# Scores of a gated recurrence: one 128 by 128 product per chunk and level, or two of 64 by 64 in two column tiles

## The chip, the cores and the metric

The kernel runs on one core of a Trainium2 chip. The metric is the device time of one execution in microseconds (us); lower is better. Before the change, three timed executions took 2496.66, 2498.34 and 2501.14 us, with a median of 2498.34 us.

## The reference

One layer of an encoder works on two requests, 256 and 1024 tokens of width 1024. Everything is held in fp32. The layer has three blocks with layer norms between them: a token mixer, a cross attention to 256 memory tokens, and a squared-ReLU MLP. The change lies in one branch of the mixer, a recurrence with four heads of width 128 that runs over the tokens in both directions. In one direction, cut to what matters:

```python
f = lb + (1 - lb) * sigmoid(zf)          # decay of each channel and token, in (0, 1)
k = 1 - f
# state: S_t = f_t * S_(t-1) + k_t v_t^T,   output: o_t = q_t S_t
scores[t, s] = sum_d q[t, d] * k[s, d] * prod(f[s+1 .. t], d)      # s <= t, inside a chunk
o = scores @ v + (q * decay) @ S_at_chunk_start
```

The other direction is the same on flipped tokens, and the two outputs are added. Then come an RMS norm over the 128 channels and a gate.

## The kernel before, in words

All 1280 tokens of both requests (T) are handled together, as ten chunks of 128 tokens (NT = 10, P = 128). Channels lie on the 128 partitions, tokens along the free dimension. The recurrent branch is the function `hgrn`. For each head h, `proj(h)` computes the projections (f for both directions, q, and for every second head the values v), and `scan(h, ...)` computes the recurrence.

`scan` cannot form `prod(f)` for each pair of tokens, so it works by levels of doubling block size B = 1, 2, 4, ... 64 (`LEVELS`). At a level, a pair of neighbouring blocks of B tokens gets the scores between its left and its right half: keys in one half, decayed to the border, times queries in the other half, decayed from the border. One arrangement serves both directions: `ka` holds for each token the key of the direction in which it is earlier (a copy on ScalarE, line 232), and `view` reads the query array `qp` with its two planes alternating every B tokens. The product of the 128 keys of a chunk with its 128 queries (line 236) gives 128 by 128 numbers, of which only those in neighbouring blocks of size B are wanted. `copy_predicated` on VectorE (line 237) writes these into `A` with a mask of the level (`masks`), for up to four chunks in one instruction (`BATCHES`: 4, 4 and 2 chunks). Before the levels, the diagonal comes from an undecayed product (line 217) that ScalarE copies into `A` whole (line 218). After the products of a level, `qp` and `ks` are multiplied on VectorE by the decays of the blocks (lines 247 and 249), and the block decays F are multiplied in pairs (line 251).

So a head has eight rounds of ten products, in fp32. In the trace TensorE shows each fp32 product as two records, each with a weight load (LDWEIGHTS) and a matrix product (MATMUL). After the levels come the states S between chunks (transposed keys, line 276; updates, line 281; additions on VectorE, lines 285 and 288), the outputs (line 300), the norm, a transpose (line 308) and the gate (line 309).

The order of work on each engine is set when the program is built: a scheduler of the tile framework (`schedule_with_timeline_sim=True`) plays the program through with times of its own and puts instructions that are ready ahead of those that are not. Here it fills TensorE between two levels with independent products: those of the gate g of the same head (line 259 evicts them), of the two large sigmoid gates (`self.gate`) and of the next head's `proj`. They are three-term products in split fp32 ("fp32r", a high and a low part of each factor), issued by the helper lines 116 to 118. Their weights are loaded by DMA, rounded on ScalarE (line 86) and split on GpSimd (line 87).

Buffers: the products of a round go to PSUM tiles `lv` (three buffers), the state products to `ms` (two buffers). `A`, `S` and the rest of a head come from the pool `hp` with one buffer each, and are used again by the next head.

Of the kernel before, what the change touches and what calls it, by code (L numbers as in the profile page):

```python
# [10 lines left out]
F32 = mybir.dt.float32  # L11
F32R = mybir.dt.float32r
F16 = mybir.dt.float16
U8 = mybir.dt.uint8
# [6 lines left out]
P = 128  # L21
# [4 lines left out]
NT = T // P  # L26
# [11 lines left out]
LEVELS = [1, 2, 4, 8, 16, 32, 64]  # L38
# [2 lines left out]
CHUNKS = [(g, c, g * GRP + c, n) for g in range(2) for c, n in GCH]  # L41
SEQS = [(0, TP // P), (TP // P, NT)]
BATCHES = [(0, 4), (4, 8), (8, 10)]
NPRE = 3
NATT = 7
HGATES = [(0, 0, (1,)), (1, 0, (0, 1)), (0, 1, (0, 1)), (1, 1, (0, 1))]
# [21 lines left out]
class Kern:  # L68
# [98 lines left out]
    def hgrn(self, xT, hp, pj, lv, ms):  # L167
        nc, a = self.nc, self.a
        masks = self.masks
# [33 lines left out]
        def scan(h, f, ks, qp, q, v):  # L203
            nka = [0]

            def new_ka():
                nka[0] += 1
                return hw[:, 6 + nka[0] % 2]

            kd = new_ka()  # L210
            A = self.t(hp, [P, NT, P], F32, "A")
            nc.vector.tensor_tensor(kd, ks[:, 0], ks[:, 1], op=ALU.add)
            nc.vector.tensor_tensor(qp, f, q.unsqueeze(1).broadcast_to([P, 2, T]), op=ALU.mult)
            for b0, b1 in BATCHES:
                ps = self.t(lv, [P, 4, P], F32, "lv")
                for c in range(b0, b1):
                    nc.tensor.matmul(ps[:, c - b0], kd[:, c * P:(c + 1) * P], q[:, c * P:(c + 1) * P], start=True, stop=True)
                nc.scalar.copy(A[:, b0:b1], ps[:, :b1 - b0])
            F, FN = f, T
            for li, B in enumerate(LEVELS):  # L220
                nb = T // (2 * B)

                def halves(x, h0, nblk=nb, B=B):
                    if B == 1:
                        return bass.AP(tensor=x.tensor, offset=x.offset + h0 * (T + 1), ap=[x.ap[0], [2, nblk]])
                    return bass.AP(tensor=x.tensor, offset=x.offset + h0 * (T + B), ap=[x.ap[0], [2 * B, nblk], [1, B]])

                def view(x, c, n=P, B=B):
                    return bass.AP(tensor=x.tensor, offset=x.offset + c * P,
                                   ap=[x.ap[0], [2 * B, n // (2 * B)], [T + B, 2], [1, B]])  # L230
                ka = new_ka()
                nc.scalar.copy(ka.rearrange("p (n h i) -> p n h i", h=2, i=B), view(ks, 0, T))
                for b0, b1 in BATCHES:
                    ps = self.t(lv, [P, 4, P], F32, "lv")
                    for c in range(b0, b1):
                        nc.tensor.matmul(ps[:, c - b0], ka[:, c * P:(c + 1) * P], view(qp, c), start=True, stop=True)  # L236
                    nc.vector.copy_predicated(A[:, b0:b1], masks[:, li].unsqueeze(1).broadcast_to([P, b1 - b0, P]),
                                              ps[:, :b1 - b0])

                def ftot(pl, half, F=F, FN=FN, B=B, nblk=nb):  # L240
                    x = F[:, pl, half:FN:2]
                    if B == 1:
                        return x
                    return x.unsqueeze(2).broadcast_to([P, nblk, B])
                for hf in range(2):
                    x = halves(qp, hf)
                    nc.vector.tensor_tensor(x, x, ftot(hf, 1 - hf), op=ALU.mult)
                    x = halves(ks, hf)
                    nc.vector.tensor_tensor(x, x, ftot(1 - hf, 1 - hf), op=ALU.mult)
                F2 = self.t(hp, [P, 2, FN // 2], F32, f"F{li % 2}")  # L250
                nc.vector.tensor_tensor(F2, F[:, :, 0:FN:2], F[:, :, 1:FN:2], op=ALU.mult)
                F, FN = F2, FN // 2

            sg = self.t(hp, [P, T], F32, "q")
            w = self.w("wh", 4 * h + 3)
            for gi, cl, c0, n in CHUNKS:
                ps = self.t(pj, [P, 512], F32, "pj")
                self.mm_t(ps[:, :n], w, xT[gi], cl, n)
                nc.scalar.activation(sg[:, c0:c0 + n], ps[:, :n], AF.Sigmoid)
                nc.vector.tensor_tensor(sg[:, c0:c0 + n], ps[:, :n], sg[:, c0:c0 + n], op=ALU.mult)  # L260

            vh = v[:, :, (h % 2) * P:(h % 2 + 1) * P]
            S = self.t(hp, [P, 2, NT - 2, P], F32, "S")
            at = [{}, {}]
            for dr in range(2):
                order = []
                for s0, s1 in SEQS:
                    cs = list(range(s0, s1))
                    if dr:
                        cs = cs[::-1]  # L270
                    order += [(c, cs[i + 1], i > 0) for i, c in enumerate(cs[:-1])]
                for g in range(0, len(order), 4):
                    grp = order[g:g + 4]
                    pt = self.t(ms, [P, 4, P], F32, "ms")
                    for j, (c, _, _) in enumerate(grp):
                        nc.tensor.transpose(pt[:, j], ks[:, dr, c * P:(c + 1) * P], self.ident)
                    kn = self.t(hp, [P, 4, P], F32, "kn", 2)
                    nc.scalar.copy(kn[:, :len(grp)], pt[:, :len(grp)])
                    pu = self.t(ms, [P, 4, P], F32, "ms")
                    for j, (c, _, _) in enumerate(grp):  # L280
                        nc.tensor.matmul(pu[:, j], kn[:, j], vh[:, c], start=True, stop=True)
                    for j, (c, nx, inner) in enumerate(grp):
                        at[dr][nx] = len(at[dr])
                        if inner:
                            nc.vector.scalar_tensor_tensor(S[:, dr, at[dr][nx]], S[:, dr, at[dr][c]], F[:, 1 - dr, c:c + 1], pu[:, j],
                                                           op0=ALU.mult, op1=ALU.add)
                        else:
                            nc.vector.tensor_copy(S[:, dr, at[dr][nx]], pu[:, j])

            ss = self.t(hp, [P, NT], F32, "ss")  # L290
            for b0, b1 in BATCHES:
                nb = b1 - b0
                po = self.t(ms, [P, 4, P], F32, "ms")
                for c in range(b0, b1):
                    terms = [(A[:, c], vh[:, c])]
                    for dr in range(2):
                        if c in at[dr]:
                            terms.append((qp[:, 1 - dr, c * P:(c + 1) * P], S[:, dr, at[dr][c]]))
                    for j, (l, r) in enumerate(terms):
                        nc.tensor.matmul(po[:, c - b0], l, r, start=j == 0, stop=j == len(terms) - 1)  # L300
                o, s_ = A[:, b0:b1], ss[:, b0:b1]
                nc.scalar.activation(o, po[:, :nb], AF.Square)
                nc.vector.tensor_reduce(s_, o, axis=AX.X, op=ALU.add)
                self.rsqrt_pow(s_, s_, 1.0 / P, nb)
                nc.vector.tensor_tensor(o, po[:, :nb], s_.unsqueeze(2).broadcast_to([P, nb, P]), op=ALU.mult)
                pt = self.t(lv, [P, 4, P], F32, "lv")
                for j in range(nb):
                    nc.tensor.transpose(pt[:, j], o[:, j], self.ident)
                nc.vector.scalar_tensor_tensor(o, pt[:, :nb], self.gn[:, 0:1], sg[:, b0 * P:b1 * P].rearrange("p (c t) -> p c t", t=P),
                                               op0=ALU.mult, op1=ALU.mult)  # L310
                nc.gpsimd.dma_start(self.o_d[h, :, b0 * P:b1 * P], o.rearrange("p c t -> p (c t)"))
# [655 lines left out]
    def run(self, stop=99):  # L967
# [13 lines left out]
        with ExitStack() as fs:  # L981
# [10 lines left out]
                        self.load_act(self.xT[g], k, a["xT"][k][:, g * GRP:(g + 1) * GRP], GRP, mp)  # L992
            with ExitStack() as hs:
                hp = hs.enter_context(tc.tile_pool(name="hp", bufs=1, reuse_waits="tile"))
                self.masks = hp.tile([P, len(LEVELS), P], U8, name="masks")
                raw = self.t(self.rawp, [P, 1024], F32, "raw")
                nm = len(LEVELS) * P
                nc.gpsimd.dma_start(raw[:, :nm], a["masks"].rearrange("p l t -> p (l t)"))
                nc.vector.tensor_copy(self.masks.rearrange("p l t -> p (l t)"), raw[:, :nm])
                self.hgrn(self.xT, hp, pj, lv, ms)  # L1000
# [37 lines left out]
def _layout(i):  # L1038
    f = np.float32
# [48 lines left out]
    r["gnorm"] = c(A["hg_gnorm"].reshape(P, 1))  # L1088
    r["ident"] = np.eye(P, dtype=f)
    ix = np.arange(P)  # L1090
    r["masks"] = c(np.stack([((ix[:, None] // b) ^ (ix[None] // b)) == 1 for b in LEVELS], 1).astype(f))
    r["wga"], r["wgb"] = tb(col["ga"]), tb(col["gb"])
    r["wpab"] = c(np.concatenate([tb(A["w_pa"][0]), tb(A["w_pb"][0])], 2))
    r["wout"] = nb(A["w_out"][0], 2, 512)
# [28 lines left out]
```

## Time and profile before

The profiled execution took 2497.39 us, and its profile spans 2495.5 us.

| What | Value |
|---|---|
| timed executions, median | 2498.34 us |
| profiled execution, its own time | 2497.39 us |
| its span | 2495.5 us |
| TensorE products (PE) busy | 2413.9 us, 97% |
| TensorE weight loads (PEld) busy | 2238.7 us, 90% |
| VectorE (DVE) busy | 1351.6 us, 54% |
| ScalarE (ACT) busy | 850.3 us, 34% |
| GpSimd (POOL) busy | 487.7 us, 20% |
| scores of the recurrence | from 170 to 558 us after the start |

Products on TensorE overlap: the profile gives each its latency, so that the sum of their times is longer than the stretch that they fill, and the distance from one start to the next is what one costs in a row of them. In the chain of waits, a piece "x20" is a run of 20 records with its length on the clock.

### The profile page before, as it was taken

The page shows a single profiled execution, that of the slowest core. Times are in us where ns is not written, and L with a number is a line of the kernel's source. Part 1 is how long each engine was busy: PE and PEld are TensorE (multiplying, and loading weights), DVE is VectorE, ACT ScalarE, POOL GpSimd, SP SyncE. Part 2 cuts the span into 40 slices and gives each one's busy share as a digit, 9 for nine tenths or more (in the row PEclk, how much of TensorE's full clock was granted, in tenths as well). Part 3 has the DMA queues.
Part 4 walks back from the last instruction along what each step waited for, and adds up shares of the span by engine and source line. Part 5 has one row for each costly group of instructions (what it writes and reads, how often), then busy time and mean ns, then how long its engine had stood idle before and what let it go on. Part 6 is the DMA issues. An engine that isn't in the chain of part 4 may idle for free.

```text
span 2495.5 us, 36014 instructions
## 1 busy us (share of the span) xinstructions
PE 2413.9 (97%) x14940; PEld 2238.7 (90%) x14940; DVE 1351.6 (54%) x2049; ACT 850.3 (34%) x1433; POOL 487.7 (20%) x423
## 2 busy tenths in 40 slices
PE   8999999999999699999999999999999999999997
PEld 6899999999978588889899999989989889999996
DVE  5136654565888585565644444457254564444435
ACT  5222222223477574324232222223222423222220
POOL 5521221214632132222100000005321210000000
PEclk9999999999999899999999999999999999999999
DMA  8611111112256587533322232335324413222211
GB/s 294 161 35 32 44 40 37 45 33 62 62 108 131 105 147 193 185 105 114 112 70 90 73 90 73 90 99 192 126 84 136 152 46 115 76 71 76 77 57 51
DMA packets 153491, 242.73 MB, mean 97 GB/s; under 512 B 85424, under 2 KB 98752, under 8 KB 152304
## 3 DMA queue, kind: packets, MB, share of 16 engines
q1 hardware_dynamic: 133424, 193.88, 27.7%
q0 software_dynamic: 19904, 46.55, 5.7%
q8 instruction: 117, 1.92, 0.3%
q14 instruction: 46, 0.38, 0.0%
HBM read 192.82 MB, written 28.05 MB: 89 GB/s over the span
## 4 chain that ended last, share of the span: by engine, by line
PE 75%; DVE 6%; DMA 4%; ACT 2%; issue 1%; POOL 0%; POOLq 0%; SPq 0%; DVEq 0%; ACTq 0%
PE a L117 9%; PE a L118 9%; PE a L116 9%; PE a L127 8%; PE a L128 8%; PE a L129 8%; PE pj L118 2%; PE pj L116 2%; PE pj L117 2%; PE lv L236 2%; DMA act<-p 1%; PE of L485 1%; PE of L116 1%; PE of L118 1%; PE of L117 1%
## 5 line engine op out<-in xcount | busy, mean ns | idle before, releaser
L116 PE MATMUL a<-act,w 128*128 128x384 f32 (+1 forms) x1664 | 513.3, 309 | 0.6 <-ACT act L86 0.6
L117 PE MATMUL a<-act,w 128*128 128x384 f32 (+1 forms) x1664 | 513.6, 309 | 0.0
L118 PE MATMUL a<-act,w 128*128 128x384 f32 (+1 forms) x1664 | 513.3, 309 | 0.0
L87 POOL TENSOR_TENSOR w<-raw,w 128x1024 fp32r<-128x1024 f32 (+2 forms) x100 | 255.0, 2552 | 558.8 <-ACT w L86 551.9
L116 PEld LDWEIGHTS a<-act,w 128*128 128x128 f32 x1664 | 315.4, 190 | 1.5 <-ACT act L86 1.0
L117 PEld LDWEIGHTS a<-act,w 128*128 128x128 f32 x1664 | 315.5, 190 | 0.7 <-DVE act L87 0.2
L118 PEld LDWEIGHTS a<-act,w 128*128 128x128 f32 x1664 | 315.2, 190 | 0.1
L86 ACT CAST w<-raw 128x1024 fp32r<-128x1024 f32 (+1 forms) x210 | 218.4, 1041 | 242.8 <-PE a L129 163.0
L116 PE MATMUL pj<-act,w 128*128 128x384 f32 (+2 forms) x688 | 220.5, 321 | 8.3 <-ACT act L86 6.3
L117 PE MATMUL pj<-act,w 128*128 128x384 f32 (+2 forms) x688 | 220.8, 321 | 2.2 <-DVE act L87 2.2
L118 PE MATMUL pj<-act,w 128*128 128x384 f32 (+2 forms) x688 | 219.2, 321 | 3.2 <-POOL w L87 3.2
L133 POOL TENSOR_SCALAR rs<-mv 128x1 f32<-128x1 f32 x30 | 17.2, 572 | 1000.0 <-DVE mv L670 999.8
L941 DVE SCALAR_TENSOR_TENSOR y<-y,a 128x512 f32<-128x512 f32 x160 | 109.6, 685 | 165.6 <-PE a L129 165.0
L127 PE MATMUL a<-w,act 128*128 128x512 f32 x480 | 187.8, 392 | 2.2 <-ACT act L86 2.2
L128 PE MATMUL a<-w,act 128*128 128x512 f32 x480 | 188.4, 393 | 0.0
L127 PE MATMUL a<-act,act 128*128 128x512 f32 x480 | 186.7, 390 | 1.6 <-ACT act L86 1.6
L129 PE MATMUL a<-w,act 128*128 128x512 f32 x480 | 187.9, 391 | 0.0
L129 PE MATMUL a<-act,act 128*128 128x512 f32 x480 | 186.9, 390 | 0.0
L128 PE MATMUL a<-act,act 128*128 128x512 f32 x480 | 186.9, 390 | 0.0
L87 DVE TENSOR_TENSOR w<-raw,w 128x1024 fp32r<-128x1024 f32 x110 | 134.6, 1223 | 61.7 <-ACT w L86 61.7
L929 DVE TENSOR_TENSOR sg<-sg 128x256 f32<-128x256 f32 (+1 forms) x128 | 62.7, 491 | 169.1 <-ACT sg L928 164.6
L86 ACT CAST act<-raw 128x1024 fp32r<-128x1024 f32 (+2 forms) x84 | 76.8, 918 | 215.8 <-PE a L129 148.7
(217 smaller groups left out, 4788.6 us busy)
## 6 DMA issues: line engine op xcount, KB each, us to landing
raw<-in_wup_dram SPq DMA_DIRECT2D x64, 512.0 KB
raw<-in_wdn_dram SPq DMA_DIRECT2D x64, 512.0 KB
raw<-in_wh_dram SPq DMA_DIRECT2D x16, 512.0 KB
raw<-in_wpab_dram SPq DMA_DIRECT2D x16, 512.0 KB
raw<-in_wout_dram SPq DMA_DIRECT2D x16, 512.0 KB
raw<-in_wxq_dram SPq DMA_DIRECT2D x16, 512.0 KB
act<-k_d POOLq DMA_DIRECT2D x8, 1024.0 KB, 6.7
act<-v_d POOLq DMA_DIRECT2D x16, 512.0 KB, 5.9
```

The lines of the kernel that those rows point to most:

```text
L86: nc.scalar.copy(hi, src)
L87: (eng or nc.vector).tensor_tensor(lo, src, hi.bitcast(F32), op=ALU.subtract)
L116: nc.tensor.matmul(ps, wh, xh, start=st, stop=False)
L117: nc.tensor.matmul(ps, wh, xl, start=False, stop=False)
L118: nc.tensor.matmul(ps, wl, xh, start=False, stop=en)
L127: nc.tensor.matmul(ps, xh, wh, start=st, stop=False)
L128: nc.tensor.matmul(ps, xh, wl, start=False, stop=False)
L129: nc.tensor.matmul(ps, xl, wh, start=False, stop=en)
L236: nc.tensor.matmul(ps[:, c - b0], ka[:, c * P:(c + 1) * P], view(qp, c), start=True, stop=True)
L485: nc.tensor.matmul(ov[:, i], vv, pt[:, x, st], start=st == 0 and x == 0, stop=st == ns - 1 and x == 1)
L929: nc.vector.tensor_tensor(r[:, :n], r[:, :n], r[:, :n], op=ALU.mult)
L941: nc.vector.scalar_tensor_tensor(y[:, i, c], y[:, i, c], ALPHA if fb == 0 else 1.0, ps, op0=ALU.mult, op1=ALU.add)
```

## The change

A chunk of 128 tokens is now treated as two halves of 64 (H2 = 64). For the diagonal and the levels B = 1 to 32, scores are wanted only inside a half. So each product is replaced by two, z = 0 and 1: 64 keys of half z as weights (128 by 64), 64 queries of the same half as the moving data, and the result goes to PSUM partitions 64z to 64z+63 and 64 columns. The start partition of the result puts the second product into the other 64 columns of the TensorE array. For B = 64, the keys of half z meet the queries of the other half.

The results of a chunk take 64 columns for 128 partitions: a PSUM tile of the same size now holds eight chunks (`HBATCH`: 8 and 2), and the scores are collected in a compact array L of ten chunks by 64 columns, with masks of half the width and six levels. L has no memory of its own; it is a view of the first 640 columns of S, which is allocated at the head's start instead of behind the levels. At the end ScalarE writes A: the blocks off the diagonal straight from the PSUM of level 64, where no mask is needed, and the two diagonal blocks from L.

```diff
+HBATCH = [(0, 8), (8, 10)]
+H2 = P // 2
...
-            for b0, b1 in BATCHES:
-                ps = self.t(lv, [P, 4, P], F32, "lv")
+
+            S = self.t(hp, [P, 2, NT - 2, P], F32, "S")
+            L = S.rearrange("p d c t -> p (d c t)")[:, :NT * H2].rearrange("p (c t) -> p c t", t=H2)
+            for b0, b1 in HBATCH:
+                ps = self.t(lv, [P, 8, H2], F32, "lv")
                 for c in range(b0, b1):
-                    nc.tensor.matmul(ps[:, c - b0], kd[:, c * P:(c + 1) * P], q[:, c * P:(c + 1) * P], start=True, stop=True)
-                nc.scalar.copy(A[:, b0:b1], ps[:, :b1 - b0])
+                    for z in range(2):
+                        x = slice(c * P + z * H2, c * P + (z + 1) * H2)
+                        nc.tensor.matmul(ps[z * H2:(z + 1) * H2, c - b0], kd[:, x], q[:, x], start=True, stop=True)
+                nc.scalar.copy(L[:, b0:b1], ps[:, :b1 - b0])
...
-                for b0, b1 in BATCHES:
-                    ps = self.t(lv, [P, 4, P], F32, "lv")
+                for b0, b1 in HBATCH:
+                    ps = self.t(lv, [P, 8, H2], F32, "lv")
                     for c in range(b0, b1):
-                        nc.tensor.matmul(ps[:, c - b0], ka[:, c * P:(c + 1) * P], view(qp, c), start=True, stop=True)
-                    nc.vector.copy_predicated(A[:, b0:b1], masks[:, li].unsqueeze(1).broadcast_to([P, b1 - b0, P]),
-                                              ps[:, :b1 - b0])
+                        for z in range(2):
+                            x = slice(c * P + z * H2, c * P + (z + 1) * H2)
+
+                            r = view(qp, c * P + z * H2) if B < H2 else qp[:, 1 - z, c * P + (1 - z) * H2:c * P + (2 - z) * H2]
+                            nc.tensor.matmul(ps[z * H2:(z + 1) * H2, c - b0], ka[:, x], r, start=True, stop=True)
+                    if B < H2:
+                        nc.vector.copy_predicated(L[:, b0:b1], masks[:, li].unsqueeze(1).broadcast_to([P, b1 - b0, H2]),
+                                                  ps[:, :b1 - b0])
+                    else:
+                        for z in range(2):
+                            rows = slice(z * H2, (z + 1) * H2)
+                            nc.scalar.copy(A[rows, b0:b1, (1 - z) * H2:(2 - z) * H2], ps[rows, :b1 - b0])
+                if B == H2:
+                    for z in range(2):
+                        rows = slice(z * H2, (z + 1) * H2)
+                        nc.scalar.copy(A[rows, :, z * H2:(z + 1) * H2], L[rows])
...
-            S = self.t(hp, [P, 2, NT - 2, P], F32, "S")
```

The order in which the instructions stand moves a little. On TensorE, at the diagonal and the first level of head 0, this stood before (line 217 the diagonal, line 236 a level, lines 116 to 118 fillers; a row with x4 is four products):

```order
L217 MATMUL lv_1393<-q_768,act_767 128x128 x4
L217 MATMUL lv_1399<-q_768,act_767 128x128 x4
L217 MATMUL lv_1405<-q_768,act_767 128x128 x2
L116 MATMUL pj_1576<-act_108,w_1573 128x256
L117 MATMUL pj_1576<-act_108,w_1573 128x256
L116 MATMUL pj_1603<-act_108,w_1573 128x384
L117 MATMUL pj_1603<-act_108,w_1573 128x384
L116 MATMUL pj_1630<-act_109,w_1573 128x256
L117 MATMUL pj_1630<-act_109,w_1573 128x256
L236 MATMUL lv_1410<-act_767 128x128 x4
L236 MATMUL lv_1416<-act_767 128x128 x4
L236 MATMUL lv_1422<-act_767 128x128 x2
```

And this stands there now (line 224 the diagonal, line 247 a level, lines 118 to 120 fillers):

```order
L224 MATMUL lv_1394<-q_768,act_767 64x64 x16
L224 MATMUL lv_1412<-q_768,act_767 64x64 x4
L247 MATMUL lv_1419<-act_767 64x64 x16
L118 MATMUL pj_1645<-act_108,w_1642 128x256
L119 MATMUL pj_1645<-act_108,w_1642 128x256
L118 MATMUL pj_1672<-act_108,w_1642 128x384
L247 MATMUL lv_1437<-act_767 64x64 x4
L119 MATMUL pj_1672<-act_108,w_1642 128x384
```

Every row of ten products became twenty of half the width, and three fillers now stand inside the first level instead of six ahead of it. Over the whole program TensorE goes 66 times from products with 128 weight columns to products with 64, or back. Before, no product had fewer than 128.

On ScalarE, behind the last level of head 0, this stood before (line 232 copies the keys, 182 a sigmoid of the next head, 278 copies the transposed keys):

```order
L232 COPY act_767<-act_767 128x1280
L182 ACTIVATE act_767<-pj_1870 128x256
L182 ACTIVATE act_767<-pj_1896 128x384
L278 COPY kn_1690<-ms_1685 128x512
L182 ACTIVATE act_767<-pj_1922 128x256
L278 COPY kn_1706<-ms_1701 128x512
```

Now the same place reads (line 239 the keys, 184 the sigmoid, 297 the transposed keys, 258 and 254 the copies into A):

```order
L239 COPY act_767<-act_767 128x1280
L184 ACTIVATE act_767<-pj_1938 128x256
L297 COPY kn_1758<-ms_1753 128x512
L258 COPY A_1390<-S_1393 64x10x64 x2
L184 ACTIVATE act_767<-pj_1964 128x384
L254 COPY A_1390<-lv_1605 64x8x64 x2
L254 COPY A_1390<-lv_1624 64x2x64 x2
L297 COPY kn_1774<-ms_1769 128x512
```

Six copies into A stand between two copies of transposed keys. The first state copy into S on VectorE (line 307 now, line 288 before) writes where L lies, and therefore comes after the two copies of line 258.

More of the change, by code (lines that the diff above doesn't have):

```diff
@@ L226, in halves, with view @@
                     return bass.AP(tensor=x.tensor, offset=x.offset + h0 * (T + B), ap=[x.ap[0], [2 * B, nblk], [1, B]])
-                def view(x, c, n=P, B=B):
-                    return bass.AP(tensor=x.tensor, offset=x.offset + c * P,
+                def view(x, t, n=H2, B=B):
+                    return bass.AP(tensor=x.tensor, offset=x.offset + t,
                                    ap=[x.ap[0], [2 * B, n // (2 * B)], [T + B, 2], [1, B]])
@@ L994, in run @@
                 hp = hs.enter_context(tc.tile_pool(name="hp", bufs=1, reuse_waits="tile"))
-                self.masks = hp.tile([P, len(LEVELS), P], U8, name="masks")
+                self.masks = hp.tile([P, len(LEVELS) - 1, H2], U8, name="masks")
                 raw = self.t(self.rawp, [P, 1024], F32, "raw")
-                nm = len(LEVELS) * P
+                nm = (len(LEVELS) - 1) * H2
                 nc.gpsimd.dma_start(raw[:, :nm], a["masks"].rearrange("p l t -> p (l t)"))
@@ L1090, in _layout @@
     ix = np.arange(P)
-    r["masks"] = c(np.stack([((ix[:, None] // b) ^ (ix[None] // b)) == 1 for b in LEVELS], 1).astype(f))
+    r["masks"] = c(np.stack([((ix[:, None] % H2 // b) ^ (ix[None, :H2] // b)) == 1 for b in LEVELS[:-1]], 1).astype(f))
     r["wga"], r["wgb"] = tb(col["ga"]), tb(col["gb"])
```

## The prediction, made before the changed kernel was run

> **What bounds the kernel now.** I read the page first: busy shares, and the span in 40 slices.
>
> ```profile
> PE 2413.9 (97%) x14940; PEld 2238.7 (90%) x14940; DVE 1351.6 (54%) x2049; ACT 850.3 (34%) x1433; POOL 487.7 (20%) x423
> ...
> PE   8999999999999699999999999999999999999997
> ```
>
> TensorE is full almost everywhere. Does that hold in the stage that the change touches? I asked for the busy time between 170 and 600 us, with the columns PE, PEld, DVE, ACT and POOL behind the length, and for TensorE's waits there.
>
> ```profile
> 265.00:273.00 8.00, 4.88 (x37) 4.67 (x35) 5.43 (x3) 4.06 (x6) 4.63 (x1) 0.95 0.00 1
> ...
> 170.00:600.00 430.00, 425.04 (x3150) 424.10 (x3149) 239.22 (x374) 113.78 (x178) 95.86 (x84) 0.99 0.13 41
> ```
>
> ```profile
> PE pj L118 <- POOL w L87: 3.2, 1, 3.2
> PE pj L116 <- DVE q L191: 1.5, 1, 1.5
> ...
> PE lv L236 <- DVE act L247: 0.3, 1, 0.3
> ```
>
> In 430 us TensorE lacks 5.0 us, and three waits explain them: 3.2, 1.5 and 0.3 us. The other engines are busy 56% (DVE) or less. Time taken from TensorE here is therefore time taken from the kernel, and time added is added.
>
> **What the changed products cost now.** The instructions that touch the tile `lv`:
>
> ```profile
> L236 PE MATMUL lv<-act x560: 272/275/415, 173.3 to 557.9; 128*128 128x128 f32 x187
> L237 DVE COPY_PREDICATED A<-masks,lv x84: 426/733/776, 175.5 to 558.4; 128x512 f32<-128x512 uint8 x56, 128x256 f32<-128x256 uint8 x28
> L217 PEld LDWEIGHTS lv<-q,act x80: 188/192/192, 170.1 to 508.6; 128*128 128x128 f32 x80
> L217 PE MATMUL lv<-q,act x80: 272/275/275, 170.2 to 508.7; 128*128 128x128 f32 x80
> ```
>
> 560 and 80 records are 280 and 40 products, two records each. Their 275 ns are latency; the cost in a row is read from the chain of waits, here for head 2 (start, length, what):
>
> ```profile
> 402.98 2.23 PE lv L217 x20
> ...
> 406.04 3.33 PE lv L236 x20
> ...
> 416.17 2.40 PE lv L236 x20
> ...
> 424.32 2.23 PE lv L236 x20
> ...
> 431.85 2.23 PE lv L236 x20
> ...
> 438.78 2.23 PE lv L236 x20
> ...
> 446.37 2.23 PE lv L236 x20
> ...
> 453.63 2.23 PE lv L236 x20
> ```
>
> A record costs 2.23/20 = 0.1115 us, at B = 2 0.120 and at B = 1, where the query view jumps at every element, 0.167. A head pays 6 x 2.23 + 2.40 + 3.33 = 19.1 us, four heads 76.4 us. This is all that can be won on TensorE. Its weight load takes 192 ns, but starts while the product ahead of it runs: records follow each other at 0.1115 us, so it is hidden.
>
> **The change, part by part.** (1) 320 products of 128 x 128 become 640 of 64 x 64, so 640 records become 1280. No row of before has such a product: the price must be bounded. If the two halves of a chunk run side by side in their column tiles, a chunk takes the time of one half: with half the columns to stream and to load, half of 76.4 is saved, **-38.2 us**. If they run one after the other, twice as many records at half the length save nothing. If a record does not get shorter, 1280 cost 152.8: +76.4 us. What a record costs beside its columns is seen in the fillers of 384 and 256 columns:
>
> ```profile
> 269.13 0.34 PE L116 MATMUL pj<-act,w 128*128 128x384 f32 x1
> 269.30 0.34 PE L117 MATMUL pj<-act,w 128*128 128x384 f32 x1
> ...
> 269.48 0.28 PE L116 MATMUL pj<-act,w 128*128 128x256 f32 x1
> 269.60 0.28 PE L117 MATMUL pj<-act,w 128*128 128x256 f32 x1
> ...
> 273.43 0.41 PE L116 MATMUL pj<-act,w 128*128 128x256 f32 x1
> 273.64 0.41 PE L117 MATMUL pj<-act,w 128*128 128x256 f32 x1
> ```
>
> Start to start, 384 columns cost 0.17 to 0.18 us and 256 cost 0.12: 128 columns are 0.05 to 0.06, so that 256 would be 0.10 to 0.11 and some 0.01 is fixed. Behind the hole at 270 us, in the stretch with the granted clock below 1, 256 columns cost 0.21: the distance follows the array's clock and hardly any fixed time, which speaks for records that shrink with their columns. For 640 more records I take 0.005 each, +3.2 us in series, **+1.6 side by side** (between 0 and 0.013, so up to 8 in series). I take "side by side" because each half has its own columns of weights and its own partitions of PSUM; between ends as far apart as -38 and +76 this is a choice, not a reading.
>
> The Trainium skill bears on it from both sides. "TensorEngine Tiling (Array Packing)", Key Properties, says that different tiles can load weights and multiply in parallel, but that a change of tiling mode drains TensorE. No run so far shows a tiled product; by the first half the saving is as above, by the second the borders below cost something.
>
> (2) The borders. The 640 products stand in blocks between full-width work, with 66 changes between 128 and 64 weight columns. Nothing of before has such a border. Below, it costs 0. Above, TensorE empties (275 of latency less the 112 ns after which the next would have started = 163 ns), and the next weight load, 192 ns, is not hidden: 0.355 us, 66 x 0.355 = 23.4 us. I take the emptying alone, the first weights being loaded meanwhile: 66 x 0.163 = **+10.8 us**.
>
> (3) VectorE and ScalarE. The groups by form, busy us and mean ns:
>
> ```profile
> L237 DVE COPY_PREDICATED A<-masks,lv 128x512 f32<-128x512 uint8 x56 | 41.2, 741 | 39.4 <-PE lv L236 39.0
> L237 DVE COPY_PREDICATED A<-masks,lv 128x256 f32<-128x256 uint8 x28 | 12.3, 440 | 0.0
> ...
> L218 ACT COPY A<-lv 128x512 f32<-128x512 f32 x8 | 4.6, 590 | 1.9 <-PE lv L217 1.9
> L218 ACT COPY A<-lv 128x256 f32<-128x256 f32 x4 | 1.5, 383 | 0.0
> ```
>
> Masked copies fall from 84 to 48: 24 of 512 elements at 0.741, and 24 of 128, which the step from 512 to 256 puts at 0.29. That is 24.7 instead of 53.5 us, -28.8 on VectorE. ScalarE loses 6.1 us and gains, per head, copies of 512 and 128 out of the diagonal (0.59 + 0.28), four out of level 64 (2 x 0.59 + 2 x 0.28) and two of 640 elements from L (0.69 each): 4.0 us, 16 in all, +10. Both engines have hundreds of idle microseconds in the stage and TensorE waits for them 1.8 us: **0**. Masks of 384 instead of 896 columns shorten one load, DMA and cast alike, ahead of the branch: 0.
>
> (4) The new order between L and S. VectorE's first state copy waits for ScalarE's two copies out of L (1.4 us), behind it stand the state additions and, in the same queue, the last decays of the queries. TensorE feels it when `ms` comes free late; 29 fillers (at 0.12 to 0.17 us, 4 us) stand ahead of the next product that needs it. Cost 0; without that cover 1.4 us in each of four heads, 5.6. The other way round, L's first copy in the next head needs S to be read out; in TensorE's order the last readers stand ahead of the diagonal, so 0.
>
> (5) The hole at 270 us is a wait for weights that GpSimd splits (3.2 us). The diagonal in front of it gets 1.1 us shorter; the wait grows by as much: **+1.0 us**. Elsewhere the levels have air: from the chain, level pieces begin at 424.32 and end at 426.55, and
>
> ```profile
> 427.10 1.56 DVE L247 TENSOR_TENSOR act<-act,F 128x640 f32<-128x640 f32 x2
> ```
>
> the queries are ready at 428.66, three microseconds before the next level starts at 431.85. A shorter level leaves this as it is.
>
> Sum: -38.2 + 1.6 + 10.8 + 1.0 = -24.8 us. The profiled execution took 2497.39 us (span 2495.5), 0.95 below the median: 2497.4 - 24.8 = 2472.6, say **2473 us**.
>
> **The rivals.**
> *In series.* Weights of two tiles share one way in, or products start only when the one ahead is through: +3.2 us, with fixed costs up to +8; 2500 to 2505. For it speaks that now every record is loaded and multiplied strictly in turn; against it, that nothing in the trace had two tiles to choose from.
> *Borders that eat the gain, the slower side.* At each of the 66 borders TensorE empties and reloads, 0.355 us; with the halves in series that is 3.2 + 23.4 = +26.6, 2524 us. With the halves side by side it is only -12, and it decides only above 38.2/66 = 0.58 us a border. In series, 0.03 us a border are enough to be seen.
> *A weight load that is no longer hidden.* If in a column tile loading and multiplying take turns, a record of half the width costs 0.056 + 0.056, the old 0.1115: +76.4, 2574 us. The 192 ns loads that start under a product speak against it for full width; for tiles nothing does.
> The Trainium skill states such a rule: "TensorE: Matmul & The Clock Gate", Part 3, lets a weight load overlap products in flight only when the row group differs, and column tiles share theirs. This trace disagrees for full-width products, where all rows are the same and PEld is 90% busy beside PE at 97%.
> *The gain runs into waits.* Levels become 1.1 us shorter, fillers run out, weights from GpSimd come late as at 270 us, and the 5.6 us of (4) appear: 0 to -15, 2482 to 2497.
>
> **How the numbers follow.** Side by side 0.46, waits 0.06, in series 0.17, borders in series 0.22, unhidden loads 0.09. A measurement of this kernel can tell some 0.2%, 5 us, from no change. Side by side and two thirds of the waits are faster: 0.50. Same: 0.12 of "in series", 0.02 of the waits: 0.14. Slower: 0.05 + 0.22 + 0.09 = 0.36. The likeliest case itself reaches from 2459 (borders free) to 2486 (borders 23.4). The range that leaves out no more than 2 in 10 goes down to 2455, where the hole of (5) closes too, and up to the border case, 2524; the unhidden loads lie outside.
>
> **What would show it.** Right: pieces of 40 records in the chain take about 1.1 to 1.3 us instead of 2.23, and starts of the two halves lie closer than 0.056 us; PE still full between 170 and 600 us and the branch ends near 570. Pieces of 2.3 us show the series, of 4.5 us the unhidden load; gaps of 0.1 to 0.4 us around the pieces are the borders. VectorE's masked copies at some 25 us and ScalarE's new copies at some 16 show step 3. New waits of `ms` on VectorE or of level products on ScalarE would refute the zeros of step 4. The forecast is wrong if the two halves do not overlap at all.

## The result

The changed kernel took 2472.08 us (median of four executions, 2469.64 to 2474.06), the kernel before 2497.5 us on the same chip (2492.16 to 2501.14). The ratio is 0.9894 with a 95% interval of 0.9881 to 0.9908: 23 to 30 us faster. The profiled execution took 2469.64 us; the one of before had taken 2497.39.

The page of the changed kernel, busy time of the engines and the span in 40 slices:

```profile
span 2467.8 us, 37270 instructions
...
PE 2385.9 (97%) x15580; PEld 2201.8 (89%) x15580; DVE 1325.8 (54%) x2013; ACT 859.7 (35%) x1453; POOL 489.0 (20%) x423
...
PE   8999999999998799999999999999999999999997
```

TensorE is as full as before, with 640 records more and 28 us less busy time. The instructions at the tile `lv` (line 224 the diagonal, 247 the levels, 249 the masked copies, 327 the last transposes of a head, 254 and 225 ScalarE's copies):

```profile
L247 PEld LDWEIGHTS lv<-act x1120: 132/138/232, 173.0 to 534.0; 128*64 128x64 f32 x187
L247 PE MATMUL lv<-act x1120: 221/222/370, 173.0 to 534.1; 128*64 128x64 f32 x187
...
L224 PE MATMUL lv<-q,act x160: 221/222/271, 171.8 to 491.3; 128*64 128x64 f32 x160
L249 DVE COPY_PREDICATED S<-masks,lv x48: 280/512/758, 174.6 to 531.0; 128x512 f32<-128x512 uint8 x24, 128x128 f32<-128x128 uint8 x24
...
L327 PE MATMUL lv<-ident,A x40: 270/272/278, 244.1 to 568.7; 128*128 128x128 f32 x40
```

A single record hardly got shorter: 222 ns instead of 275. That is latency. What a round costs is its place on the clock. The last transposes show where the branch ends: the last of them starts at 568.7 us, where before it started at 592.6:

```profile
L308 PE MATMUL lv<-ident,A x40: 270/272/273, 250.2 to 592.6; 128*128 128x128 f32 x40
```

The first product of the scores stands at 171.8 us, and stood at 170.2: the work ahead of it, 912 records of TensorE in both, took 1.6 us longer in this execution. So the branch takes 396.9 us instead of 422.4, 25.5 less. The spans differ by 27.7, since behind the branch another 3.8 us are won. Most of these lie between 1000 and 1100 us, in work that the change does not touch. There the kernel before ran a stretch at a lower clock and the changed one did not, as the third column from the right shows (first the row of before, then that of the changed kernel):

```profile
1000.00:1100.00 100.00, 96.23 (x517) 85.39 (x515) 64.86 (x101) 30.99 (x44) 29.43 (x19) 0.97 0.41 132
```

```profile
1000.00:1100.00 100.00, 95.23 (x523) 84.61 (x522) 54.46 (x86) 25.86 (x38) 27.00 (x22) 1.00 0.36 114
```

I read both, the 1.6 and the 3.8, as scatter between executions; the kernel before alone scatters over 9 us.

The level rounds in the timeline of TensorE, a block of level 4 in head 1 between its neighbours (start, length with the last latency, what):

```profile
286.53 0.34 PE L119 MATMUL pj<-act,w 128*128 128x384 f32 x1
286.80 1.39 PE L247 MATMUL lv<-act 128*64 128x64 f32 x40
288.12 0.44 PE L120 MATMUL pj<-act,w 128*128 128x384 f32 x1
288.40 0.28 PE L118 MATMUL pj<-act,w 128*128 128x256 f32 x1
```

1.39 less the 0.22 of the last record's latency leaves 1.17 us for 40 records, 0.029 each, where the twenty of before took 2.23. At one instant inside the block eight records are in flight:

```profile
287.14 0.41 PE L247 MATMUL lv<-act 128*64 128x64 f32 x8
```

Record by record, the starts in the trace come in pairs 0.007 us apart, one pair every 0.058 us. I read a pair as one record of each column tile; the first experiment, where neighbours share a tile, has single starts at the same distance. From 286.53 to 288.40 are 1.87 us. Two fillers of 0.175 and a round of 1.17 are 1.52; the remaining 0.35 us are two borders, 0.175 us each.

What TensorE waits for between 160 and 600 us is nearly what it was:

```profile
PE pj L120 <- POOL w L89: 3.9, 3, 3.5
PE pj L118 <- DVE q L193: 0.7, 1, 0.7
PE lv L224 <- DVE q L193: 0.2, 1, 0.2
```

VectorE's masked copies and ScalarE's copies by form:

```profile
L249 DVE COPY_PREDICATED S<-masks,lv 128x512 f32<-128x512 uint8 x24 | 17.9, 744 | 95.7 <-PE lv L247 95.7
...
L249 DVE COPY_PREDICATED S<-masks,lv 128x128 f32<-128x128 uint8 x24 | 6.9, 289 | 0.0
```

```profile
L258 ACT COPY A<-S 64x640 f32<-64x640 f32 x8 | 5.8, 726 | 2.3 <-DVE S L249 2.2
...
L254 ACT COPY A<-lv 64x512 f32<-64x512 f32 x8 | 4.6, 581 | 8.7 <-PE lv L247 8.6
...
L225 ACT COPY S<-lv 128x512 f32<-128x512 f32 x4 | 2.4, 588 | 2.5 <-PE lv L224 2.4
...
L254 ACT COPY A<-lv 64x128 f32<-64x128 f32 x8 | 2.1, 260 | 0.1
...
L225 ACT COPY S<-lv 128x128 f32<-128x128 f32 x4 | 1.1, 275 | 0.0
```

They sum to 24.8 and 16.0 us, where the forecast had 24.7 and 16.

### The profile page after: what moved, and what is told of

The parts are those of the page before. It is cut to its first block, busy times and chain, and to the rows that moved or that the text cites. A ratio compares the mean times of both kernels' runs of the same rounds, so it can differ in the third digit from the quotient of the medians.

```text
span 2467.8 us, 37270 instructions
## 1 busy us (share of the span) xinstructions
PE 2385.9 (97%) x15580; PEld 2201.8 (89%) x15580; DVE 1325.8 (54%) x2013; ACT 859.7 (35%) x1453; POOL 489.0 (20%) x423
## 4 chain that ended last, share of the span: by engine, by line
PE 73%; DVE 7%; DMA 5%; ACT 2%; issue 2%; POOL 1%; POOLq 0%; SPq 0%; DVEq 0%; ACTq 0%
PE a L119 9%; PE a L120 9%; PE a L118 9%; PE a L131 8%; PE a L130 8%; PE a L129 8%; PE pj L120 2%; PE pj L118 2%; PE pj L119 2%; DMA act<-p 1%; PE of L504 1%; PE lv L247 1%; PE of L118 1%; PE of L120 1%; PE of L119 1%
```

## The experiments

The theory after the result: the two halves of a chunk overlap in TensorE because neighbouring products go to different column tiles; each border costs some 0.17 us; nothing else counts. Rivals: the gain comes from cheaper records as such, or from VectorE; the borders are free. In the following, a ratio is always to the kernel before in the same job.

**Halves in a row.** The same products in another order, so that neighbours share a tile:

```diff
-                    for c in range(b0, b1):
-                        for z in range(2):
+                    for z in range(2):
+                        for c in range(b0, b1):
```

> The same products, evacuations and borders as the changed kernel (2472 us); only the loops over chunks and halves are exchanged, so that all products of one half of a PSUM tile stand together, eight or two in a row, and then all of the other half. Theory (two tiles run side by side when neighbouring records go to different tiles): the overlap is gone but for one place in a block; a run of 40 records takes about 2.3 us instead of 1.22, in all 33 blocks some 35 us more: 2507 us, about 10 over the kernel before (ratio 1.004). Rival (the gain lies in cheaper records or in less work for VectorE and needs no alternation): nothing changes, 2472 us (ratio 0.990).

Measured: 2493.97 us, ratio 0.9984 (0.9970 to 0.9998). Most of the gain is gone, 0.9984 - 0.9894 = 0.009, or 22 us of the 26. A block of level 4 (head 1) in the timeline:

```profile
291.85 0.34 PE L119 MATMUL pj<-act,w 128*128 128x384 f32 x1
292.11 2.13 PE L247 MATMUL lv<-act 128*64 128x64 f32 x40
294.18 0.45 PE L120 MATMUL pj<-act,w 128*128 128x384 f32 x1
```

2.13 less 0.22 is 1.91 us instead of 1.17. The overlap of neighbouring tiles is what the change lives on: same products, same columns, same evacuations, same number of borders. In the middle of a run in one tile only four records are in flight, where the changed kernel had eight:

```profile
292.40 0.40 PE L247 MATMUL lv<-act 128*64 128x64 f32 x4
```

Their starts lie 0.058 us apart, one by one. A half-width record in its tile thus costs a little more than half of a full one (0.1115/2 = 0.056), and 39 such steps would be the 2.3 us that I expected. The block is shorter because the overlap at a change of tile reaches further than one record: around each of the three changes the trace has several pairs of starts 0.004 to 0.006 us apart, and each change saves some 0.12 us, about two records.

**Full-width products behind and between.** To price the borders, 112 useless products of 128 x 128 were added to the 28 level rounds, once behind the round and once inside it:

```diff
+                    for _ in range(4 if b0 else 0):
+                        nc.tensor.matmul(ps[:, 4:6], ka[:, :P], self.ident, start=True, stop=True)
```

```diff
                     for c in range(b0, b1):
+                        if c in (2, 4, 6, 8):
+                            nc.tensor.matmul(ps[:, 6:8] if c < 8 else ps[:, 4:6], ka[:, :P], self.ident, start=True, stop=True)
```

> Control for the next run: the changed kernel with four more full-width fp32 products (128 x 128, their results are not used) behind each of the 28 level rounds, 112 in all. They stand behind the round's last small product, so the number of borders between 128 and 64 weight columns stays at 66. Both theories: 112 products of two records at 0.1115 us are 25 us, 2472 + 25 = 2497 us.

> The same 112 extra products, but standing inside the rounds, between the chunks 2, 4, 6 and 8 and the ones ahead of them: 286 borders instead of 66. Theory (a border costs about 0.145 us, as the starts around the blocks in the changed kernel's trace show): 220 more borders are 32 us more than the control, about 2529 us. Rival 1 (borders are free, the gaps are only how starts are stamped): the same as the control, 2497 us. Rival 2 (a border empties and reloads TensorE at 0.355 us): 78 us more, 2575 us.

Measured behind: 2494.41 us, ratio 0.9978 (0.9963 to 0.9993). Between: 2536.93 us, ratio 1.0152 (1.0129 to 1.0175). The control stands 0.0084, or 21 us, above the changed kernel, near the 25 expected for its products. The same work in another place costs 0.0174 of 2500 us, 43 us more, or 0.20 us for each of the 220 borders; by the ends of the intervals 0.15 to 0.24. The timeline of the kernel with the products between shows one step by step:

```profile
194.11 0.45 PE L249 MATMUL lv<-act 128*64 128x64 f32 x8
194.49 0.49 PE L244 MATMUL lv<-ident,act 128*128 128x128 f32 x2
194.91 0.45 PE L249 MATMUL lv<-act 128*64 128x64 f32 x8
195.29 0.49 PE L244 MATMUL lv<-ident,act 128*128 128x128 f32 x2
```

A period is 0.80 us. Eight small records at 0.029 are 0.23 and two large ones 0.22: 0.35 us are left for two borders, as in the changed kernel itself. Free borders and the full emptying with a reload (0.355 each) are both out. The price that I had derived from the stamps before this run, 0.145, was too low, since I had charged the round 0.05 us too much.

**VectorE's saving given back.** Each masked copy of a level stands twice:

```diff
                         nc.vector.copy_predicated(L[:, b0:b1], masks[:, li].unsqueeze(1).broadcast_to([P, b1 - b0, H2]),
                                                   ps[:, :b1 - b0])
+                        nc.vector.copy_predicated(L[:, b0:b1], masks[:, li].unsqueeze(1).broadcast_to([P, b1 - b0, H2]),
+                                                  ps[:, :b1 - b0])
```

> The changed kernel with every masked copy of the levels done twice in a row (the second changes nothing): VectorE gets back the 24.8 us that the compact array saved there (24 copies at 0.744 and 24 at 0.289). Theory (TensorE alone sets the time of this stage): 2472 us, ratio to the kernel before 0.989 as without it. Rival (part of the gain came from VectorE): up to 25 us more, 2497 us, ratio 0.999.

Measured: 2475.01 us, ratio 0.9907 (0.9881 to 0.9933). The rival's 0.999 lies outside the interval, and the interval holds the ratio of the changed kernel. By its upper end the interval would still hide some 10 us. The profile is narrower: between 160 and 640 us TensorE waits 1.7 us for VectorE, and 0.9 in the changed kernel. So the masked copies save VectorE half its work there, and next to nothing of it reaches the time.

**Memory of its own for L.**

```diff
-            L = S.rearrange("p d c t -> p (d c t)")[:, :NT * H2].rearrange("p (c t) -> p c t", t=H2)
+            L = self.t(hp, [P, NT, H2], F32, "L")
```

> The changed kernel with memory of its own for the compact array L, so that the first state copies into S no longer wait for ScalarE's copies out of L. Theory (that wait is covered by fillers on TensorE): 2472 us, ratio 0.989. Rival (the wait costs its 1.4 us in each head): 5.6 us less, 2466 us, ratio 0.987.

Measured: 2474.1 us, ratio 0.9901 (0.9877 to 0.9926). Nothing is gained. The interval still holds 0.987, so the time alone does not rule out the 5.6 us; the profile does for the branch. TensorE's waits between 160 and 640 us are those of the changed kernel to 0.1 us, and none of them is for `ms`; the longest:

```profile
PE pj L120 <- POOL w L89: 3.9, 3, 3.5
PE pq L129 <- ACT qn L394: 1.0, 1, 1.0
PE pj L118 <- DVE q L193: 0.7, 1, 0.7
```

**Four column tiles.** If the mechanism is right, it can be used again. Below level 32, scores are wanted only inside 32 tokens:

```diff
+            L = S.rearrange("p d c t -> p (d c t)")[:, :NT * H4].rearrange("p (c t) -> p c t", t=H4)
+            ps = self.t(lv, [P, 16, H4], F32, "lv")
+            for c in range(NT):
+                for z in range(4):
+                    x = slice(c * P + z * H4, c * P + (z + 1) * H4)
+                    nc.tensor.matmul(ps[z * H4:(z + 1) * H4, c], kd[:, x], q[:, x], start=True, stop=True, tile_position=(0, z * H4))
+            nc.scalar.copy(L, ps[:, :NT])
```

> The step taken once more: the diagonal and the levels 1 to 16 as four products of 32 keys with 32 queries in four column tiles, collected in an array of ten chunks by 32; level 32 becomes four unmasked products of neighbouring quarters that ScalarE copies into A, as level 64 does with halves; level 64 stays. 66 borders as before. Theory (tiles run side by side, each record as long as its columns): seven of eight rounds fall from 1.22 to about 0.62 us, 4 x (6 x 0.6 + 0.8) = 17 us less, 2455 us. Rival 1 (only two records are ever in flight, or starts have a floor of some 0.03 us a pair): rounds of 80 records stay at 1.2 us, 2472 us. Rival 2 (ScalarE's eight more small copies a head, 4 us, get into TensorE's way): above 2472 us.

Measured: 2463.26 us, ratio 0.9862 (0.9846 to 0.9878): faster than with two tiles, but by 8 us instead of 17. Both rivals are out: their 2472 us or more, a ratio of 0.990, lies above the interval, and a round does not stay at 1.2 us. A round in the timeline, and the products of the levels by the view of the tile (least, mean and greatest latency in ns):

```profile
299.05 0.28 PE L119 MATMUL pj<-act,w 128*128 128x256 f32 x1
299.26 0.90 PE L247 MATMUL lv<-act 128*32 128x32 f32 x80
300.08 0.39 PE L120 MATMUL pj<-act,w 128*128 128x256 f32 x1
```

```profile
L247 PE MATMUL lv<-act x1920: 189/196/263, 177.8 to 522.1; 128*32 128x32 f32 x192
```

0.90 less the 0.20 of the last record leaves 0.70 us for 80 records instead of the 1.17 of the 40 before; over 28 rounds this is 13 us. The 0.62 of the forecast for a round would have taken a record down to 0.008 us; it is 0.009. In the trace four records, as I read it one for each tile, start within 0.032 to 0.034 us. A record in its tile so costs 0.1115, 0.058 and 0.032 us at 128, 64 and 32 columns: some 0.005 us of it do not shrink with the columns (an estimate from these three), and a round does not fall by half.

But TensorE now waits more (160 to 620 us):

```profile
PE pj L121 <- POOL w L90: 7.2, 3, 3.6
PE of L119 <- ACT w L89: 1.6, 1, 1.6
PE lv L224 <- DVE q L194: 0.5, 1, 0.5
```

The gain starts to run into the weights from GpSimd: three times they come late, where before and with two tiles it was once for long. With each of the three waits, the granted clock falls too (windows of 5 and 6 us that begin in the wait, third column from the right):

```profile
181.00:186.00 5.00, 4.24 (x44) 4.01 (x47) 3.60 (x4) 1.26 (x1) 0.71 (x1) 0.66 0.50 185
270.00:275.00 5.00, 3.90 (x19) 3.85 (x19) 2.47 (x2) 0.00 (x0) 1.05 (x1) 0.66 0.28 105
395.00:401.00 6.00, 4.71 (x100) 4.49 (x100) 4.60 (x5) 1.26 (x1) 1.24 (x1) 0.72 0.49 171
```

At a mean of 0.66, 0.66 and 0.72, each window gives up about 1.7 us of full clock (0.34 x 5 and 0.28 x 6). With two tiles the one long wait had a mean of 0.62 in the 9 us from 266 to 275, or 3.4 us of full clock. Four tiles thus lose some 1.7 us more to the clock and 3.3 more to the waits themselves (7.2 against 3.9), about the 5 us between the 13 of the rounds and the 8 measured. That the wait lowers the clock is so far read from its place alone.

**The late weights asked for earlier.** What is late are the weights of a head's gate g. They are requested inside `scan`, behind three others, and so, by the order of requests, get the buffer that comes free last. With one line, they stand in front:

```diff
             gb = HGATES[h]
+            self.w_ahead(("wh", 4 * h + 3))
             self.w_ahead(("wga" if gb[0] == 0 else "wgb", gb[1]))
```

> The changed kernel, but the gate weights of a head (the ones that TensorE waits for once, 3.5 us, at the start of head 1, with 6.8 us at half clock behind it) are asked for before the two weights of the next head and the large gate instead of behind them, so that they take a buffer that comes free earlier. Nothing is computed otherwise. Theory (the hole is a wait for a late weight buffer): the wait falls away, 3.5 us and half of 6.8 us less: 2465 us, ratio 0.986. Rival (another load then comes late in its place): 2472 us or more, ratio 0.989.

> The four column tiles of the earlier run (2463 us, ratio 0.986, where TensorE waited three times for these weights, 7.2 us in all, each with a stretch of 3.4 us at half clock) together with the earlier request for the gate weights. Theory (its rounds saved some 14 us of TensorE and the waits took back 9): waits and half-clock stretches fall away, 2463 - 7 - 3 x 1.7 = 2451 us, ratio 0.981. Rival (the loss lies elsewhere): 2463 us, ratio 0.986.

With two tiles: 2467.75 us, ratio 0.9882 (0.9844 to 0.9920). The wait for GpSimd is gone from the profile:

```profile
PE pj L118 <- DVE q L193: 1.5, 1, 1.5
PE pq L129 <- ACT qn L395: 1.1, 1, 1.1
PE pq L130 <- POOL w L89: 0.2, 1, 0.2
```

but the interval holds both the expected 0.986 and the 0.989 without it: as a time, inconclusive. With four tiles: 2452.34 us, ratio 0.9819 (0.9790 to 0.9848), as the theory expected. That is 11 us below four tiles alone, 45 us below the kernel before, and the fastest of all versions here. Its waits:

```profile
PE S L425 <- ACT rr L422: 2.1, 2, 2.0
PE pq L130 <- ACT qn L404: 1.1, 1, 1.1
PE lv L247 <- DVE act L276: 0.2, 1, 0.2
```

With the waits the low clock is gone too. The granted clock between 160 and 640 us is 1.00 with two tiles and with four (first and second row, third column from the right), where it was 0.99 in both without the earlier request:

```profile
160.00:640.00 480.00, 477.12 (x4366) 465.90 (x4365) 273.95 (x483) 158.77 (x269) 138.69 (x134) 1.00 0.15 46
160.00:640.00 480.00, 476.33 (x5589) 465.82 (x5589) 281.15 (x485) 170.95 (x305) 146.02 (x143) 1.00 0.15 48
```

The low clock thus went when the waits for these weights went. It does not follow every wait of this length: the 2.0 us of `S` in the list above end at 639.8 us, and the granted clock from 637 to 647 us is 1.00. What decides between the two stays open.

## Why the prediction was right

The forecast was 2473 us, by a sum of -24.8 us; measured were 2472.08 and -25.4 between the medians. The mechanism and the sizes held, but that the two agree to 0.6 us is luck: the kernel before alone scatters over 9 us, and two terms of the sum are each off by some 0.7 us and cancel, the borders and the hole.

**What bounds the kernel** was read rightly: TensorE, in this stage nearly alone. Giving VectorE its work back changed nothing that the runs can tell; taking the overlap from TensorE took most of the gain.

**Step 1**, the halves side by side, held with its size. The forecast of -38.2 + 1.6 = -36.6 us says 39.8 us for all rounds. Measured are 1.17 us for six rounds of a head, 1.25 for level 2 and 1.64 for level 1 (head 3), from the first start to the last: 9.9 us a head, 39.6 in all. The 0.005 us for each additional record held as well, since two half records take 0.116 us in their tile and one full record 0.1115. That the halves overlap was a choice when the prediction was made, and the order of halves and chunks shows that it is the cause. The Trainium skill's page "TensorEngine Tiling (Array Packing)", Key Properties, states that different tiles can load weights and multiply in parallel, and that a change of tiling mode drains TensorE. The runs agree with the first by 1.17 us against 1.91 for the same products in another order; of the second they show a price, not the draining.

**Step 2**, the borders, held too: 0.163 us was forecast for each, 0.175 is read in the trace, 0.20 (0.15 to 0.24) follows from the times. 66 of them give back 11 to 13 of some 37 us. That it is the emptying of the array is an explanation that fits the size; the runs show the price, not what happens inside.

**Step 3** was right in sum and effect. **Step 4** was right as far as the waits show it. **Step 5** had the mechanism and a wrong size: the hole at head 1 grew by 0.3 us (3.2 to 3.5), not by 1.0. In both traces the late weights come 6.6 us after the start of the last filler ahead of the diagonal of head 1 (266.49 to 273.05 before, 261.06 to 267.63 now), so the wait does grow by what the diagonal gets shorter. But from that filler to the second one behind it, the diagonal took 2.52 us before and takes 2.23 now, 0.3 less and not 1.1. The step left out the diagonal's own two borders (0.35 us), and could not know that a wait of 0.2 us for VectorE now breaks its round in two.

**The rivals.** "In series" had about the right price, +3.2 us: by the starts in one tile, 640 pairs of half records cost 640 x (0.116 - 0.1115) = 2.9 us more than 640 full ones. It did not come, and even the kernel with halves in a row does not run fully in series, as its changes of tile show; by its ratio it is 0.5 to 7.5 us faster than the kernel before, borders included. The "borders" rival had too high a price (0.355). Two ends of the likeliest case are not what the sum's own terms give: with free borders these make 2462 us, not 2459, and with borders of 23.4 us 2485, not 2486. "A weight load that is no longer hidden" fell: it put a half record at 0.1115 us, and in its tile it takes 0.058. In the trace's records weight loads of 138 ns overlap products in all column tiles, although these share their rows. The Trainium skill's page "TensorE: Matmul & The Clock Gate", Part 3, has a load overlap products in flight only if the row group differs; these records do not bear that out. "The gain runs into waits" came one step later than asked: not with two tiles, but with four, for the weights it had named.

## What to carry to other kernels

Where masks throw away most of a product on a full TensorE, small products in column tiles are worth it, if neighbours in the order go to different tiles; the same products in the wrong order gave almost nothing. Count the borders between full-width and tiled work, here 0.17 to 0.2 us each, and keep tiled products in long blocks. When the bounding engine gets faster, look at what it waits for next before the next step: with four tiles, one earlier weight request was worth about as much (11 us) as the step from two tiles to four had been (8 us); with two tiles its effect was too small to be told from none.

## What was not expected

Where neighbours in the order change their tile, the overlap reaches over several records: I had expected 2.3 us for a block with its halves in a row, and it took 1.91. With four tiles a round fell by 40% (1.17 to 0.70 us), not by half. The starts lie 0.009 us apart on average there, far closer than within a tile, but the part of a record that does not shrink, some 0.005 us, weighs more in a record of 0.032 us than in one of 0.058.
